# Linear attention on one core: a loop over groups becomes a loop over pairs, with work placed between the cells of an output

## The chip, the cores and the metric

The kernel runs on one core of a Trainium2 chip. The core has a matrix engine (TensorE, PE in the profile), a vector engine (VectorE, DVE), a scalar engine (ScalarE, ACT), a general engine (GpSimd, POOL) and a sync engine (SyncE, SP) that here only issues DMAs. Each engine works through its own list of instructions in order and waits on semaphores for the others. The metric is the device time of one execution in microseconds (us); the number quoted is a median of runs.

## The reference

```python
batch, heads, seq, dim = 8, 12, 512, 64      # Q, K, V: float32

Q_feat = np.maximum(0, Q) + 1
K_feat = np.maximum(0, K) + 1
KV = np.einsum('bhkd,bhkv->bhdv', K_feat, V)
K_sum = np.sum(K_feat, axis=2)
numerator = np.einsum('bhqd,bhdv->bhqv', Q_feat, KV)
denominator = np.einsum('bhqd,bhd->bhq', Q_feat, K_sum)
return (numerator / (denominator[:, :, :, None] + 1e-10)).astype(np.float32)
```

There are 96 heads. For each, a 64 x 64 matrix KV and a 64-vector K_sum are summed over 512 keys, and then every one of 512 queries is multiplied with both and divided.

## The kernel before

**Tiling.** The 49152 rows of Q, K and V are cut into 12 groups (`NG`), numbered 0 to 11; two neighbouring groups, an even one and the odd one behind it, form a pair, and there are six pairs. Loads convert from float32 to bf16 on the way in. From the second pair on, K, V and Q of a pair come as one DMA each, and each of the three has two buffers (`IN_BUFS`), so the load for pair s+2 waits until pair s has been read out of its buffer. All these loads and ten of the twelve stores are issued by GpSimd, in the order of the program; the stores of groups 10 and 11 are issued by SyncE, group 11's in five pieces (`store`, lines 133 to 150). The outputs of a pair share one of five buffers `o_sb`; the first load of Q also uses one.

**The steps for one group.** *k features* and *q features* (`feature`, line 153): max(x+1, 1) on VectorE, two instructions each. *V blocks* (`v_blocks`, lines 164 to 172): four copies of V, each multiplied with a 0/1 mask column, so that heads that share a tile stay apart; VectorE makes two and a half of the four (three instructions, line 170), ScalarE one and a half (two instructions, line 172). *Keys-values* (`keys_values`, line 194): 64 matmuls of k features with V blocks into psum tiles `kva_ps`. These sum over the pair, and behind the odd group four *kva copies* on ScalarE (line 207) bring them to bf16 in SBUF. *Transposes* (`transposes`, line 220): 16 on TensorE, eight to each of two psum tiles `qt_ps`, of which there are two in all; two *qt copies* (line 223) bring them to SBUF. The transposes of the even group fill columns 0 to 3 of the pair's `qt` tile, those of the odd group columns 4 to 7. *Output* (`out_matmuls`, line 233): per group two halves h, each with two output tiles `o_ps` of eight matmuls; the first tile of a half reads columns 0 to 3 of `qt`, the second 4 to 7, so both groups of a pair need the transposes of both. There are two `o_ps` tiles in all. *Norms* (`norms`, lines 250 and 251): VectorE takes the reciprocals of the denominators and multiplies, 48 times each in the whole kernel.

**What sets the order.** The order is written by hand: inside `tc.manual_schedule()` each engine executes what concerns it in the order of the program text, and the framework only adds the semaphore waits. The loop at line 290 runs over groups 0 to 9; groups 10 and 11 are written out at lines 310 to 327. In a round for an even group a stand k features and V blocks of a, the output of a-2, q features of a and of a+1, and keys-values of a. In the round for the odd group b = a+1 stand the transposes and qt copies of a, k features and V blocks of b, the output of a-1, the transposes and qt copies of b, keys-values of b and the kva copies. GpSimd's DMA issues for the next pair but one come behind the odd group; the stores begin with the round for group 7.

Of the kernel before, what the change touches and what calls it, by code (L numbers as in the profile page):

```python
# [19 lines left out]
def kernel(  # L20
# [27 lines left out]
    W = 2 * D1  # L48
# [31 lines left out]
    raw = {}  # L80
    bufs = {}
    kfs = {}
    qfs = {}
    qts = {}
    outs = {}
    cells_of = {}
    kva_ps = {}

    def load_first_q():
# [38 lines left out]
    def load_pair(s):  # L128
        load("k", (2 * s, 2 * s + 1))
        load("v", (2 * s, 2 * s + 1))  # L130
        load_q(s)
# [25 lines left out]
    def k_features(g):  # L157
        k_raw = raw.pop(("k", g))
        kf = kf_pool.tile([P, C2, 2, D], BF16, name="kf")
        for n in range(2):  # L160
            feature(kf[:, :, n], k_raw[:, n])
        kfs[g] = kf

    def v_blocks(g):
        v_raw = raw.pop(("v", g))
        for b in range(4):
            block = v_all[:, g % 2, :, :, b, 0:D]
            cut = 2 if b < 2 else 1 if b == 2 else 0
            if cut > 0:
                nc.vector.tensor_scalar_mul(block[:, 0:cut], v_raw[:, 0:cut], mask[:, b : b + 1])  # L170
            if cut < 2:
                nc.scalar.mul(out=block[:, cut:], in_=v_raw[:, cut:], mul=mask[:, b : b + 1])  # L172

    def q_features(g):
        q_raw = raw.pop(("q", g))
        qf = qf_pool.tile([P, R, C // 2, 2, D], BF16, name="qf")
        for n in range(2):
            feature(qf[:, :, :, n], q_raw[n])
        qfs[g] = qf

    def keys_values(g):
        kf = kfs.pop(g)
        if g % 2 == 0:
            kva_ps[g // 2] = [psum_kva.tile([P, BANK], FP32, name="kva_ps") for _ in range(2)]
        halves = kva_ps[g // 2]
        for c in range(C2):
            for n in range(2):
                if g < 2:
                    eight, first, last_c = g, (c, n) == (0, 0), (c, n) == (C2 - 1, 1)
                else:  # L190
                    eight, first, last_c = n, g % 2 == 0 and c == 0, g % 2 == 1 and c == C2 - 1
                for h in range(2):
                    ps = slice(64 * h, 64 * h + 64)
                    nc.tensor.matmul(  # L194
                        halves[h][64 * eight : 64 * eight + 64, 0 : 4 * DV],
                        lhsT=kf[ps, c, n, :],
                        rhs=v_all[ps, g % 2, n, c],
                        start=first,
                        stop=last_c,
                    )  # L200
        if g % 2 == 0:
            return
        for h in range(2):
            kva = kva_diag[(g - 1 + h) % NV]
            for n in range(2):
                ps = slice(64 * n, 64 * n + 64)
                nc.scalar.copy(  # L207
                    out=kva[ps, :, n, :],
                    in_=halves[h][ps, 0 : 4 * DV].rearrange("p (b x) -> p b x", b=4)[:, :, 0:D1],
                )  # L210

    def transposes(g):
        qf = qfs.pop(g)
        if g % 2 == 0:
            qts[g // 2] = mid_pool.tile([P, C, P, R], BF16, name="qt")
        for half in range(2):
            qt_ps = psum_qt.tile([P, 2, R, P], BF16, name="qt_ps")
            for c in range(2):
                for r in range(R):
                    nc.tensor.transpose(qt_ps[:, c, r], qf[:, r, 2 * half + c, :, :], identity)  # L220
            copy = nc.vector.tensor_copy if half and g == NG - 2 else nc.scalar.copy
            lo = g % 2 * 4 + 2 * half
            copy(out=qts[g // 2][:, lo : lo + 2], in_=qt_ps.rearrange("p c r q -> p c q r"))  # L223

    def out_matmuls(g, h):
        qt = qts[g // 2]
        kva = kva_diag[(g // 2 * 2 + h) % NV]
        ops = [psum.tile([P, 2, BANK], FP32, tag="ps", name="o_ps") for _ in range(2)]
        for c in range(C):
            for j in range(2):  # L230
                b = 2 * (g % 2) + j
                q = 16 * (4 * h + b)
                nc.tensor.matmul(  # L233
                    ops[c // 4][64 * j : 64 * j + 64, c // 2 % 2, (c % 2) * W : (c % 2) * W + W],
                    lhsT=qt[:, c, q : q + 16, :],
                    rhs=kva[:, b],
                    start=True,
                    stop=True,
                )
        cells_of[g, h] = ops  # L240

    def norms(g, h):
        ops = cells_of.pop((g, h))
        if (g % 2, h) == (0, 0):
            outs[g // 2] = out_pool.tile([P, 2 * NP, C, D], FP32, name="o_sb")
        o_sb = outs[g // 2]
        for i in range(2):
            cells = ops[i][:, :, 0 : 2 * W].rearrange("p b (c n x) -> p b c n x", n=2, x=D1)
            recip = recip_pool.tile([P, 2, 2, 2, 1], FP32, name="recip")
            nc.vector.reciprocal(out=recip, in_=cells[:, :, :, :, D:D1])  # L250
            nc.vector.tensor_tensor(  # L251
                out=o_sb[:, 2 * h + g % 2 : 2 * NP : NP, 4 * i : 4 * i + 4].rearrange(
                    "p n (b c) d -> p b c n d", b=2
                ),
                in0=cells[:, :, :, :, 0:D],
                in1=recip.to_broadcast([P, 2, 2, 2, D]),
                op=ALU.mult,
            )

    def output(g):  # L260
        for h in range(2):
            out_matmuls(g, h)
            norms(g, h)

    with tc.manual_schedule():
        q_first = load_first_q()
        load("k", (0,))
        load("v", (0,))
        load_rest_q(q_first)
        load("k", (1,))  # L270
        load("v", (1,))
        make_identity(nc, identity)
        nc.vector.tensor_reduce(  # L273
            out=mask,
            in_=identity.rearrange("p (h b x) -> p b h x", h=2, b=4),
            op=ALU.add,
            axis=mybir.AxisListType.XY,
        )
        for i in range(2):
            t = v_all[:, i].rearrange("p n c b x -> p (n c) b x")  # L280
            nc.vector.memset(t[:, :, :, D1:], 0.0)
            nc.vector.tensor_copy(  # L282
                out=t[:, :, :, D], in_=mask[:, None, :].to_broadcast([P, 2 * C2, 4])
            )
        for t in kva_diag:
            for b in range(4):
                nc.gpsimd.memset(t[:, b], 0.0)  # L287
        load_pair(1)
        last = NG - 1
        for g in range(last - 1):  # L290
            if g % 2:
                transposes(g - 1)
            k_features(g)
            v_blocks(g)
            if g >= 2:
                output(g - 2)
            if g % 2:
                transposes(g)
            else:
                q_features(g)  # L300
                q_features(g + 1)
            keys_values(g)
            if g % 2 and g // 2 + 2 < NG // 2:
                load_pair(g // 2 + 2)
            if g == NG - 5:
                for done in range(g - LAG):
                    store(done)
            if g >= NG - 5:
                store(g - LAG)
        k_features(last - 1)  # L310
        output(last - 3)
        out_matmuls(last - 2, 0)
        v_blocks(last - 1)
        k_features(last)
        v_blocks(last)
        keys_values(last - 1)
        store(last - 1 - LAG)
        q_features(last - 1)
        q_features(last)
        norms(last - 2, 0)  # L320
        transposes(last - 1)
        out_matmuls(last - 2, 1)
        norms(last - 2, 1)
        transposes(last)
        keys_values(last)
        output(last - 1)
        output(last)
        for g in range(last - LAG, NG):
            store(g)


# [28 lines left out]
```

## Time and profile before

| | |
|---|---|
| time, median of 3 runs | 126.53 us (126.38 to 130.75) |
| profiled execution | 126.8 us, span 125.0 us |
| TensorE, matmuls | 72.0 us busy, 58% of the span |
| VectorE | 82.4 us, 66% |
| ScalarE | 67.8 us, 54% |
| GpSimd | 24.6 us, 20% |
| HBM traffic | 37.75 MB read, 12.58 MB written: 403 GB/s over the span |
| keys-values matmuls (line 194) | 768, mean 340 ns |
| V blocks on ScalarE (line 172) | 24, mean 1572 ns |
| qt copies on ScalarE (line 223) | 23, mean 1016 ns |
| kva copies (line 207) | 24, mean 374 ns |
| norms on VectorE (lines 250, 251) | 48 of 199 ns and 48 of 692 ns |

The span is the time from the first to the last event of one profiled execution; the device time includes what lies around it, here 1.8 us. The page divides the span into 40 slices of 3.1 us and gives the busy share of each engine in each slice as a digit in tenths; for TensorE there is a second row with the clock that was granted, in tenths of full speed. The chain that ended last is followed back from the last instruction, at each step to what released it. The timeline lists merged instructions with start and length; in square brackets stands how long the engine had been idle before and what ended that.

### The profile page before, as it was taken

How to read it: one execution, taken by the hardware profiler on the slowest of the kernel's cores; microseconds unless marked ns; L12 is line 12 of the kernel's file. 1: busy time of each engine (PE TensorE's matmuls, PEld its weight loads, DVE VectorE, ACT ScalarE, POOL GpSimd, SP SyncE). 2: the span in 40 equal slices, each digit the busy share in tenths (PEclk: the TensorE clock that was granted, in tenths of full speed). 3: DMA queues.
4: the chain of work that ended last, by engine and by line, in shares of the span. 5: the costliest groups of instructions: out<-in, count | busy, mean ns of one | idle time of the engine just before them, and what ended most of it. 6: DMA issues, size and time to landing. Idle time of an engine off the chain costs nothing.

```text
span 125.0 us, 3095 instructions
## 1 busy us (share of the span) xinstructions
PE 72.0 (58%) x1344; PEld 60.9 (49%) x1344; DVE 82.4 (66%) x186; ACT 67.8 (54%) x72; POOL 24.6 (20%) x52
## 2 busy tenths in 40 slices
PE   0000297389549474696737967449767459974500
PEld 0000296289338463684626847348656337763300
DVE  0466642205299996969959769599290999939920
ACT  0006703970673989329994099870698990571000
POOL 6990020040002050020400203950201020020000
PEclk9999999855999999769995599965799955999655
DMA  3999999999999999999999999999999999999892
GB/s 86 339 214 210 219 211 216 214 211 219 211 215 215 216 212 215 215 218 214 211 218 214 211 221 208 215 215 215 216 372 414 413 418 418 409 415 413 337 372 101
DMA packets 8902, 32.18 MB, mean 257 GB/s; under 512 B 568, under 2 KB 824, under 8 KB 8760
## 3 DMA queue, kind: packets, MB, share of 16 engines
q0 software_dynamic: 7520, 28.84, 93.7%
q1 hardware_dynamic: 1368, 3.15, 7.0%
q8 instruction: 10, 0.16, 0.5%
q14 instruction: 4, 0.03, 0.1%
HBM read 37.75 MB, written 12.58 MB: 403 GB/s over the span
## 4 chain that ended last, share of the span: by engine, by line
ACT 37%; PE 33%; DVE 15%; DMA 7%; issue 3%; POOL 1%; ACTq 0%; POOLq 0%
PE kva_ps L194 28%; ACT v_all L172 24%; ACT qt L223 8%; DVE o_sb L251 7%; DMA v_raw<-in_V_dram 7%; ACT kva_all L207 4%; PE qt_ps L220 4%; DVE v_all L170 3%; DVE recip L250 2%; DVE qf L153 1%; ACT L172 1%; DVE qt L223 1%; PE o_ps L233 1%; DVE kf L153 1%; POOL k_raw L113 1%
## 5 line engine op out<-in xcount | busy, mean ns | idle before, releaser
L194 PE MATMUL kva_ps<-v_all,kf 64*64 64x272 bf16 x768 | 39.1, 340 | 25.4 <-ACT v_all L172 24.1
L194 PEld LDWEIGHTS <-kf 64*64 64x64 bf16 x768 | 35.2, 132 | 27.0 <-DVE v_all L170 13.9
L223 ACT COPY qt<-qt_ps 128x1024 bf16<-128x1024 bf16 x23 | 22.2, 1016 | 27.2 <-PE qt_ps L220 27.2
L172 ACT ACTIVATE v_all<-v_raw,mask 128x1024 bf16<-128x1024 bf16 (+1 forms) x24 | 36.4, 1572 | 0.1
L251 DVE TENSOR_TENSOR o_sb<-o_ps,recip 128x512 f32<-128x512 f32 x48 | 33.2, 692 | 1.6
L233 PE MATMUL o_ps<-kva_all,qt 128*64 128x130 bf16 x384 | 19.3, 233 | 20.1 <-DVE recip L250 7.6
L170 DVE TENSOR_SCALAR v_all<-v_raw,mask 128x2048 bf16<-128x2048 bf16 (+1 forms) x36 | 22.7, 688 | 8.5 <-DMA v_raw<-in_V_dram 8.5
L233 PEld LDWEIGHTS <-qt 128*64 128x64 bf16 x384 | 13.3, 114 | 26.3 <-DVE o_sb L251 10.6
L250 DVE RECIPROCAL recip<-o_ps 128x8 f32<-128x8 f32 x48 | 9.6, 199 | 17.3 <-PE o_ps L233 17.3
L220 PE MATMUL qt_ps<-identity,qf 128*128 128x128 bf16 x192 | 14.8, 235 | 1.1 <-ACT qt L223 1.0
L220 PEld LDWEIGHTS <-qf 128*128 128x128 bf16 x192 | 12.4, 106 | 4.0 <-issue 3.1
L207 ACT CAST kva_all<-kva_ps 64x260 bf16<-64x260 f32 x24 | 9.0, 374 | 7.4 <-PE kva_ps L194 7.1
L137 POOL DMA_DIRECT2D out_dram<-o_sb x10 | 7.5, 763 | 25.3 <-DVE o_sb L251 20.5
L153 DVE TENSOR_SCALAR kf<-k_raw 128x1024 bf16<-128x1024 bf16 x24 | 9.1, 422 | 4.7 <-DMA k_raw<-in_K_dram 4.7
L110 POOL DMA_DIRECT2D k_raw<-in_K_dram x5 | 3.6, 727 | 33.8 <-DVE kf L153 33.8
L110 POOL DMA_DIRECT2D v_raw<-in_V_dram x5 | 4.0, 793 | 26.6 <-ACT v_all L172 26.6
L153 DVE TENSOR_SCALAR qf<-q_raw 128x1024 bf16<-128x1024 bf16 x22 | 8.0, 419 | 0.1
L172 ACT ACT_TABLE_LOAD x1 | 1.3, 1283 | 10.5 <-DMA v_raw<-in_V_dram 10.5
L123 POOL DMA_DIRECT2D q_raw<-in_Q_dram x5 | 3.6, 720 | 0.0
L273 DVE TENSOR_REDUCE mask<-identity 128x4 f32<-128x128 bf16 x1 | 0.3, 286 | 4.7 <-POOL identity masks.py:199 4.7
L287 POOL MEMSET kva_all<- 128x130 bf16 x16 | 2.4, 196 | 0.0
L282 DVE CAST v_all<-mask 128x128 bf16<-128x128 f32 x2 | 2.2, 1637 | 0.0
(12 smaller groups left out, 7.2 us busy)
## 6 DMA issues: line engine op xcount, KB each, us to landing
out_dram<-o_sb POOLq DMA_DIRECT2D x10, 1024.0 KB, 20.2
k_raw<-in_K_dram POOLq DMA_DIRECT2D x5, 1024.0 KB, 14.2
v_raw<-in_V_dram POOLq DMA_DIRECT2D x5, 1024.0 KB, 13.5
q_raw<-in_Q_dram POOLq DMA_DIRECT2D x5, 1024.0 KB, 17.2
o_sb<-in_Q_dram SPq DMA_DIRECT2D x1, 1024.0 KB, 4.8
k_raw<-in_K_dram POOLq DMA_DIRECT2D x2, 512.0 KB, 9.5
v_raw<-in_V_dram POOLq DMA_DIRECT2D x2, 512.0 KB, 11.4
out_dram<-o_sb SPq DMA_DIRECT2D x1, 1024.0 KB, 5.3
```

The lines of the kernel that those rows point to most:

```text
L110: nc.gpsimd.dma_start(out=t, in_=drams[x][:, 2 * s : 2 * s + 2])
L137: nc.gpsimd.dma_start(out=o_to[:, g % 2 : 2 * NP : 2], in_=outs[s][:, g % 2 : 2 * NP : 2], single_packet=True)
L153: nc.vector.tensor_scalar(out=dst, in0=src, scalar1=1.0, scalar2=1.0, op0=ALU.add, op1=ALU.max)
L170: nc.vector.tensor_scalar_mul(block[:, 0:cut], v_raw[:, 0:cut], mask[:, b : b + 1])
L172: nc.scalar.mul(out=block[:, cut:], in_=v_raw[:, cut:], mul=mask[:, b : b + 1])
L194: nc.tensor.matmul(halves[h][64 * eight : 64 * eight + 64, 0 : 4 * DV], lhsT=kf[ps, c, n, :], rhs=v_all[ps, g % 2, n, c], start=first, sto ...
L207: nc.scalar.copy(out=kva[ps, :, n, :], in_=halves[h][ps, 0 : 4 * DV].rearrange("p (b x) -> p b x", b=4)[:, :, 0:D1],)
L220: nc.tensor.transpose(qt_ps[:, c, r], qf[:, r, 2 * half + c, :, :], identity)
L223: copy(out=qts[g // 2][:, lo : lo + 2], in_=qt_ps.rearrange("p c r q -> p c q r"))
L233: nc.tensor.matmul(ops[c // 4][64 * j : 64 * j + 64, c // 2 % 2, (c % 2) * W : (c % 2) * W + W], lhsT=qt[:, c, q : q + 16, :], rhs=kva[:, ...
L250: nc.vector.reciprocal(out=recip, in_=cells[:, :, :, :, D:D1])
L251: nc.vector.tensor_tensor(out=o_sb[:, 2 * h + g % 2 : 2 * NP : NP, 4 * i : 4 * i + 4].rearrange("p n (b c) d -> p b c n d", b=2), in0=cell ...
```

## The change

The loop over groups becomes a loop over pairs (`iteration`). The copies that followed a step inside its function (`kva copies`, `qt copies`) become functions of their own, `v_blocks` takes the engine as an argument, and `output` issues its four tiles one by one, with room for other work between them: behind the first two tiles of the output of the preceding odd group stand the transposes and qt copies of the even group, behind the third tile a quarter of the keys-values matmuls of the odd group. The q features of the odd group move behind that output and behind its own keys-values matmuls. The k features and V blocks of the next even group are issued at the end of a round; the qt copies of the preceding odd group are issued at the start of the next. In the last pair (`end`) the k features and V blocks of group 11 come first, and the qt copies of group 10 are issued behind the kva copies. The qt copy that VectorE made for group 10 is made by ScalarE. Stores 0 to 5 are issued behind the fourth pair's round, 6 and 7 behind the fifth's, 8 and 9 behind the sixth's.

```diff
-    def keys_values(g):
-        kf = kfs.pop(g)
-        if g % 2 == 0:
+    def keys_values(g, lo=0, hi=C2):
+        kf = kfs[g]
+        if g % 2 == 0 and lo == 0:
             kva_ps[g // 2] = [psum_kva.tile([P, BANK], FP32, name="kva_ps") for _ in range(2)]
         halves = kva_ps[g // 2]
-        for c in range(C2):
+        for c in range(lo, hi):
...
-        if g % 2 == 0:
-            return
+
+    def keys_values_copies(s):
+        halves = kva_ps[s]
         for h in range(2):
-            kva = kva_diag[(g - 1 + h) % NV]
+            kva = kva_diag[(2 * s + h) % NV]
...
+        qt_ps[g] = [psum_qt.tile([P, 2, R, P], BF16, name="qt_ps") for _ in range(2)]
         for half in range(2):
-            qt_ps = psum_qt.tile([P, 2, R, P], BF16, name="qt_ps")
             for c in range(2):
                 for r in range(R):
-                    nc.tensor.transpose(qt_ps[:, c, r], qf[:, r, 2 * half + c, :, :], identity)
-            copy = nc.vector.tensor_copy if half and g == NG - 2 else nc.scalar.copy
+                    nc.tensor.transpose(qt_ps[g][half][:, c, r], qf[:, r, 2 * half + c, :, :], identity)
+
+    def transpose_copies(g):
+        for half, t in enumerate(qt_ps.pop(g)):
             lo = g % 2 * 4 + 2 * half
-            copy(out=qts[g // 2][:, lo : lo + 2], in_=qt_ps.rearrange("p c r q -> p c q r"))
+            nc.scalar.copy(out=qts[g // 2][:, lo : lo + 2], in_=t.rearrange("p c r q -> p c q r"))
...
+    def output(g, between=()):
+
+        cells = [(g, h, i) for h in range(2) for i in range(2)]
+        for k in range(4):
+            if k >= 2:
+                norms(*cells[k - 2])
+                if k - 2 < len(between):
+                    between[k - 2]()
+            out_matmuls(*cells[k])
+        norms(*cells[2])
+        norms(*cells[3])
+
+    def iteration(s):
+
+
+        a, b = 2 * s, 2 * s + 1
+        end = b == NG - 1
+        quarter = C2 // 4
+        if end:
+            k_features(b)
+            v_blocks(b, "dve")
+            v_blocks(b, "act")
+        transpose_copies(a - 1)
+        output(a - 2)
+        q_features(a)
+        if end:
+            q_features(b)
+        else:
+            k_features(b)
+            v_blocks(b, "dve")
+            v_blocks(b, "act")
+        keys_values(a)
+
+        def first():
+            transposes(a)
+            if not end:
+                transpose_copies(a)
+
+        output(a - 1, (first, lambda: keys_values(b, 0, quarter)))
+        keys_values(b, quarter, C2)
+        if not end:
+            q_features(b)
+        keys_values_copies(s)
+        if end:
+            transpose_copies(a)
+        transposes(b)
+        if end:
+            transpose_copies(b)
...
+        blocks(0)
+        keys_values(0)
+        q_features(0)
+        q_features(1)
+        transposes(0)
+        blocks(1)
+        transpose_copies(0)
+        keys_values(1)
+        keys_values_copies(0)
+        transposes(1)
+        load_pair(2)
+        blocks(2)
+        for s in range(1, NG // 2):
+            iteration(s)
+            if s + 2 < NG // 2:
+                load_pair(s + 2)
+            if 2 * s + 2 < NG:
+                blocks(2 * s + 2)
+            for g in range(2 * s - 2, 2 * s) if s > 3 else range(2 * s) if s == 3 else ():
+                store(g)
+        output(NG - 2)
+        output(NG - 1)
+        for g in range(NG - 2, NG):
             store(g)
```

`blocks(g)` calls `k_features(g)`, `v_blocks(g, "dve")` and `v_blocks(g, "act")`.

More of the change, by code (lines that the diff above doesn't have):

```diff
@@ L86 @@
     cells_of = {}
+    qt_ps = {}
     kva_ps = {}
@@ L162, in k_features, with v_blocks @@
         kfs[g] = kf
-    def v_blocks(g):
-        v_raw = raw.pop(("v", g))
+    def v_blocks(g, engine):
+        v_raw = raw["v", g]
         for b in range(4):
@@ L168, in v_blocks @@
             cut = 2 if b < 2 else 1 if b == 2 else 0
-            if cut > 0:
+            if engine == "dve" and cut > 0:
                 nc.vector.tensor_scalar_mul(block[:, 0:cut], v_raw[:, 0:cut], mask[:, b : b + 1])
-            if cut < 2:
+            if engine == "act" and cut < 2:
                 nc.scalar.mul(out=block[:, cut:], in_=v_raw[:, cut:], mul=mask[:, b : b + 1])
@@ L215, in transposes, with out_matmuls @@
             qts[g // 2] = mid_pool.tile([P, C, P, R], BF16, name="qt")
+        qt_ps[g] = [psum_qt.tile([P, 2, R, P], BF16, name="qt_ps") for _ in range(2)]
         for half in range(2):
-            qt_ps = psum_qt.tile([P, 2, R, P], BF16, name="qt_ps")
             for c in range(2):
                 for r in range(R):
-                    nc.tensor.transpose(qt_ps[:, c, r], qf[:, r, 2 * half + c, :, :], identity)
-            copy = nc.vector.tensor_copy if half and g == NG - 2 else nc.scalar.copy
+                    nc.tensor.transpose(qt_ps[g][half][:, c, r], qf[:, r, 2 * half + c, :, :], identity)
+    def transpose_copies(g):
+        for half, t in enumerate(qt_ps.pop(g)):
             lo = g % 2 * 4 + 2 * half
-            copy(out=qts[g // 2][:, lo : lo + 2], in_=qt_ps.rearrange("p c r q -> p c q r"))
-    def out_matmuls(g, h):
+            nc.scalar.copy(out=qts[g // 2][:, lo : lo + 2], in_=t.rearrange("p c r q -> p c q r"))
+    def out_matmuls(g, h, i):
         qt = qts[g // 2]
         kva = kva_diag[(g // 2 * 2 + h) % NV]
-        ops = [psum.tile([P, 2, BANK], FP32, tag="ps", name="o_ps") for _ in range(2)]
-        for c in range(C):
+        o_ps = psum.tile([P, 2, BANK], FP32, tag="ps", name="o_ps")
+        for c in range(4 * i, 4 * i + 4):
             for j in range(2):
@@ L233, in out_matmuls @@
                 nc.tensor.matmul(
-                    ops[c // 4][64 * j : 64 * j + 64, c // 2 % 2, (c % 2) * W : (c % 2) * W + W],
+                    o_ps[64 * j : 64 * j + 64, c // 2 % 2, (c % 2) * W : (c % 2) * W + W],
                     lhsT=qt[:, c, q : q + 16, :],
@@ L239, in out_matmuls @@
                 )
[L240 to L244, printed above, removed]
-            outs[g // 2] = out_pool.tile([P, 2 * NP, C, D], FP32, name="o_sb")
[L246 to L263, printed above, removed]
+        cells_of[g, h, i] = o_ps
+    def norms(g, h, i):
+        cells = cells_of.pop((g, h, i))[:, :, 0 : 2 * W].rearrange(
+            "p b (c n x) -> p b c n x", n=2, x=D1
+        )
+        if (g % 2, h, i) == (0, 0, 0):
+            outs[g // 2] = out_pool.tile([P, 2 * NP, C, D], FP32, name="o_sb")
+        recip = recip_pool.tile([P, 2, 2, 2, 1], FP32, name="recip")
+        nc.vector.reciprocal(out=recip, in_=cells[:, :, :, :, D:D1])
+        nc.vector.tensor_tensor(
+            out=outs[g // 2][:, 2 * h + g % 2 : 2 * NP : NP, 4 * i : 4 * i + 4].rearrange(
+                "p n (b c) d -> p b c n d", b=2
+            ),
+            in0=cells[:, :, :, :, 0:D],
+            in1=recip.to_broadcast([P, 2, 2, 2, D]),
+            op=ALU.mult,
+        )
@@ L265, with blocks @@
+    def blocks(g):
+        k_features(g)
+        v_blocks(g, "dve")
+        v_blocks(g, "act")
     with tc.manual_schedule():
@@ L288 @@
         load_pair(1)
[L289 to L328, printed above, removed]
+        blocks(0)
[21 more added lines that the diff above has]
+        for g in range(NG - 2, NG):
             store(g)
```

## The prediction

> **What bounds the kernel now.** First the page's part 2, to see whether the transfers or the engines set the pace.
>
> ```profile
> PEclk9999999855999999769995599965799955999655
> DMA  3999999999999999999999999999999999999892
> GB/s 86 339 214 210 219 211 216 214 211 219 211 215 215 216 212 215 215 218 214 211 218 214 211 221 208 215 215 215 216 372 414 413 418 418 409 415 413 337 372 101
> ```
>
> The sixteen DMA engines are busy in every slice from the second to the thirty-seventh. Loads write 215 GB/s of bf16, that is 430 GB/s read, until about 91.3 us; then stores run at about 414 GB/s. Twelve stores of 1024 KB (1.049 MB) cost 2.53 us each, 30.4 us together, so transfers alone would end at 91.3 + 30.4 = 121.7 us. The span is 125.0. So there is a floor close beneath this kernel, and a second bound, the engines, that ends at nearly the same time. Next the chain that ended last, over one regular pair:
>
> ```profile
> 64.10 3.05 ACT v_all L172 x2
> 67.14 0.04 issue
> 67.19 3.84 PE kva_ps L194 x64
> 71.03 0.98 PE qt_ps L220 x8
> 72.01 0.02 issue
> 72.03 1.93 ACT qt L223 x2
> 73.96 2.95 ACT v_all L172 x2
> 76.91 0.04 issue
> 76.95 2.10 PE kva_ps L194 x64
> ...
> 80.21 0.38 ACT kva_all L207
> ```
>
> Columns: start, length, what. This is a loop between ScalarE and TensorE: V blocks of the even group, its 64 keys-values matmuls, the transposes, their two copies, V blocks of the odd group, its 64 matmuls, the four kva copies. It returns at 48.2, 64.1, 80.6 and 97.1 us, so a pair takes 16.5 us, against 3 x 4.88 = 14.6 us for its three loads (2.10 MB read each at 430 GB/s). Compute falls behind the loads and is the bound by the end. The timeline shows what lies beside the chain: the odd group's two qt copies run during its matmuls and cost nothing.
>
> ```profile
> 76.79 1.92 ACT L223 COPY qt<-qt_ps 128x1024 bf16<-128x1024 bf16 x2
> 76.95 2.05 PE L194 MATMUL kva_ps<-v_all,kf 64*64 64x272 bf16 x64 [0.73 <-ACT v_all L172]
> ...
> 118.80 0.69 DVE L251 TENSOR_TENSOR o_sb<-o_ps,recip 128x512 f32<-128x512 f32 x1
> 119.52 0.34 SPq L146 DMA_DIRECT2D out_dram<-o_sb  x1
> ```
>
> The last product ends at 119.5, and the pieces of the last store take 5.5 us from there to the end of the span.
>
> **The change, part by part.** No arithmetic goes or comes, except that one qt copy moves from VectorE (1.21 us) to ScalarE (1.01). What changes is the order on each in-order engine. ScalarE per pair now has: V blocks of the even group a (issued at the end of the round before), qt copies of the preceding odd group, V blocks of the odd group b, qt copies of a, kva copies. I call T the moment when the four kva copies of a pair end and follow one round from there; "cell" is an output tile of 8 matmuls (0.42), followed by a norm on VectorE of 0.84 (97.05 to 97.89).
>
> Round at the clock 1.00. ScalarE: V blocks of a to T+3.05, qt copies of a-1 to T+5.0 (0.96 each once both are pipelined). TensorE: cell 0 of group a-2 is early, since it needs only the kva copies and the even qt; cell 1 reads qt columns 4 to 7, the odd group's, so it waits until T+5.05. Norm 1 ends at T+6.2, cell 3 needs that psum tile and ends at T+6.65, and only behind it in TensorE's queue stand the matmuls of a. Before, they began at T+3.1. That is the added wait: 3.5 us, and the V blocks, done at T+3.05, wait for TensorE instead of the other way. Matmuls of a: 2.05, to T+8.7. Two cells of a-1: 0.65, T+9.35. Sixteen transposes: 1.07, T+10.4. VectorE meanwhile has norms 2 and 3 to T+7.85, q features 0.71, k features 0.67, V blocks 1.8: T+11.05; then norm 0 to T+11.9, which releases cell 2, T+12.4; a quarter of b's matmuls 0.51, T+12.9; cell 3, T+13.3 (norm 1 done at T+12.75); the other three quarters 1.54, T+14.85; kva copies 1.55 and 0.05 to start: T+16.45. Removed from the chain, in exchange: V blocks of b (2.95) now end at T+8.0, and qt copies of a run beside cells and matmuls. So the round is 16.45 at full clock, no gain on 16.5, though before's round had its first 64 matmuls at 3.84.
>
> The clock decides what is added to that. In the trace TensorE fell to 0.50 at about 24.4 after an idle stretch from 23.3, and near 65.5, 82.6 and 99.5 after the sparse output cells; it came back 3.3 to 5.5 us after dense matmuls began. In the new round TensorE does nothing from about T+0.2 to T+4.05. I take the half clock for a's matmuls alone: 3.84 brings them to T+10.5, cells T+11.15, transposes T+12.2, cell 2 T+12.65, and the round 16.7; with half of the transposes slowed too, 16.9, which I use. Bounds: 16.45, nothing slow; 19.1, everything slow (1.62 for transposes, 3.84 for both groups).
>
> The Trainium skill ("TensorE: Matmul & The Clock Gate", section "What's actually happening") says that the array's clock is halved after an idle window of about 3.4 us and released after as long a busy one. The new round's 3.85 us of idleness per pair would by that rule make a's matmuls slow in every round, where the chain of before had one round of 14.35 without it; the rule speaks against this change, and the stretches named above partly bear it out, since the clock there fell after less idleness. By it the sum is the forecast's; without it, the full-clock rival's.
>
> Start. The V blocks of group 1 no longer wait behind the qt copies of group 0: ScalarE runs them when their load is in, 17.9 to 20.9, not 22.5 to 25.5. The 64 matmuls follow at 21.1 (6.63, as slow as before) to 27.7, kva copies to 29.3. The next V blocks need the load that before had at 28.79, so T of pair 0 is 29.0, where it was 33.8: 4.8 us earned. Four rounds of 16.9 give T of pair 4 = 96.6; before had 97.1. The head start is spent.
>
> End. Before, this T to the last norm took 22.4 us (97.1 to 119.5). Now: V blocks of 10 and of 11 stand on ScalarE ahead of the qt copies of 9: 5.97 + 1.93, T+7.9. Cell 1, norm 1 and cell 3 of group 8 then end at T+9.55 (before, its matmuls of 10 began at T+5.15). Matmuls 3.84: T+13.4. Two cells T+14.05, transposes 1.07 T+15.1, cell 2 T+15.5, quarter T+16.0, cell 3 T+16.45, rest T+18.0, kva copies T+19.6. The qt copies of 10 stand behind these: 1.93, T+21.55; only they free the psum tiles for the transposes of 11, T+22.1, whose copies end at T+23.5. Before, both pairs of copies lay ahead of the kva copies. Cell 1 of group 10 needs the last copy: its norm ends T+24.7, two more norms T+26.4, four of group 11 T+29.75. Bounds: 28.0 at full clock, 31.6 at half.
>
> Sum: 96.6 + 29.75 = 126.35 for the last product, +5.5 for the store pieces = 131.85 span. The profiled execution took 126.8 around a span of 125.0, 1.8 outside: 133.65. It stands 0.27 above the median of the runs, 126.53, so **133.4** on the median's scale.
>
> Moved DMAs. GpSimd's order of loads stays. K of pair 5 is issued after k features of 7, at T(2)+9.2 = 72.0 (before 69.6); the engines need it at 91.3 - 14.6 = 76.7, so it is covered. Q of pair 5 now waits for q features that come after a whole output: T(2)+15.2 = 78.0, before 77.9; queued behind it are stores 0 to 5, needed at 91.3. Were that cover gone, each us late would be a us of idle transfers, but the end would not see it while compute ends at 126. Store 8 is issued near T+10.8 = 107.4, store 9 near 114.5, stores 10 and 11 on SP after their norms. The output buffer of group 10 needs stores 0 and 1 landed, near 98; its norms come at 119.
>
> **The rivals.** Full clock: with 16.45 and 28.0 the last product comes at 29.0 + 65.8 + 28.0 = 122.8, time 129.8. For it: matmuls spread over the round; against: the idle 3.85 us. Colder: rounds of 17.5 and an end of 31 give 130.0, time 137. For it: the clock needed up to 5.5 us of dense work to return, and cells break the dense run.
>
> The other side, **the transfer floor**: the 4.8 us earned at the start are kept because a round is no longer than its loads. Then compute follows the loads, the stores never lack data, and the end is 121.7 plus about 1.8 of landing and closing: span 123.5, time 125.0, not slower. It decides if the last product comes by 118, so T(4) by 88.3, rounds of 14.8. For it: before's first round took 14.35 at full clock, and VectorE's work per pair is only 13.1 us. Against: the wait for the odd qt copies and norm 1 ahead of the matmuls. That the order isn't as written is excluded, since the instruction lists of both kernels show it.
>
> The Trainium skill ("DMA: Bandwidth & Descriptors", section "Where 436 GB/s comes from") puts the ports' ceiling at about 435 GB/s and HBM's share per core at about 358; the loads here read 430, so the first agrees and the second doesn't. By 435 the 50.3 MB take 115.7 us, an estimate, and the floor rival would fall by some 2.8 us (88.1 of loads and 30.4 of stores in the rows).
>
> **How the numbers follow.** Forecast (131 to 136) 0.56; full clock (129 to 131) 0.14; colder (over 136) 0.12; the head start and the tail nearly cancel (124.5 to 128.5, the floor rival and part way to it) 0.14; below that 0.04. About 2% is what a measurement of this kernel can tell from no change: 124.0 to 129.1. Faster 0.04, within 0.13, slower 0.83. The range reaches from 128.5, under the full-clock end, to 137.5, past colder.
>
> **What would show it.** Right: kva copies end near 29 and then every 16.5 to 17.5 us; before the matmuls of even groups TensorE waits for ScalarE's qt copies and VectorE's norms, not V blocks; the four last qt copies end some 4 us behind the last kva copies; transfers idle after about 114; the last product near 126. Wrong: rounds of 15 or less, or cell 1 not waiting for the odd copies; then the stores end last.

## The result and the profile after

The changed kernel takes 135.1 us (median of four executions, 134.07 to 136.45). The ratio to the kernel before is 1.066, 95% interval 1.054 to 1.077: slower. The profiled execution took 134.07 us around a span of 132.3, where before it was 126.8 around 125.0. Some executions run 2 to 3.5% longer than the others of the same kernel (before up to 130.75 us, against 126.38); ratios here compare executions without that, while the times are medians of all.

Part 2 of the page of the changed kernel, as shown of before:

```profile
PEclk9999999985569995599955999558996557977755
DMA  3999999999999999999999999999999999570492
GB/s 111 316 208 217 216 212 212 214 217 216 214 217 207 219 214 214 216 211 214 216 214 216 212 217 213 214 218 284 419 417 417 417 416 410 223 307 0 165 381 91
```

The loads run as before. The stores begin as before too, but now the transfers run dry: half a slice of work at 112 to 116 us, and nothing at all in the slice around 120. The engines, which had ended level with the transfers, end behind them. The windows of this profile between the ends of the kva copies of one pair and the next, and then to the last product (columns: stretch, its length, TensorE busy, its weight loads, VectorE, ScalarE, GpSimd, granted clock, DMA share, GB/s):

```profile
26.98:45.63 18.65, 11.19 (x224) 8.55 (x224) 13.73 (x32) 11.33 (x12) 2.15 (x3) 0.73 1.06 215
45.63:62.46 16.83, 11.23 (x224) 8.60 (x224) 12.94 (x31) 11.33 (x12) 2.15 (x3) 0.80 1.06 214
62.46:79.18 16.72, 11.21 (x226) 8.66 (x224) 12.89 (x31) 11.32 (x12) 2.45 (x4) 0.80 1.06 215
79.18:96.08 16.90, 11.61 (x230) 8.66 (x224) 13.43 (x31) 11.33 (x13) 6.12 (x8) 0.80 1.05 271
96.08:116.17 20.09, 10.36 (x202) 7.86 (x201) 11.85 (x28) 9.40 (x11) 1.51 (x2) 0.75 0.94 383
116.17:126.71 10.54, 6.10 (x80) 4.20 (x79) 6.62 (x16) 3.87 (x4) 0.00 (x0) 0.72 0.43 173
```

Where the 7.3 us of span come from can be read off these six rows and the profile of before. The first kva copies end at 27.0 instead of 33.8. Four rounds later the lead is down to 1.0 us (96.1 against 97.1). The last pair takes 20.1 us where before it took 15.9 (97.1 to 113.0): 4.2 lost. From the last kva copies to the last product it is 10.5 where it was 6.5 (113.0 to 119.5): 4.0 lost. The store pieces take 5.6 us behind the last product, before 5.5. Together -1.0 + 4.2 + 4.0 + 0.1 = 7.3. The last kva copies of before, in its timeline:

```profile
111.41 1.54 ACT L207 CAST kva_all<-kva_ps 64x260 bf16<-64x260 f32 x4 [0.82 <-PE kva_ps L194]
```

What fills a round shows in the chain that ended last, here the round that began at 62.46 (start, length, what; the rows "issue" between them, 0.02 to 0.04 us each, are left out):

```profile
62.48 3.04 ACT v_all L173 x2
65.54 1.94 ACT qt L227 x2
67.52 0.45 PE o_ps L237 x4
67.99 0.22 DVE recip L253
68.24 0.70 DVE o_sb L254
68.98 0.65 PE o_ps L237 x8
69.63 3.60 PE kva_ps L195 x59
```

V blocks of the even group, then the qt copies of the odd group before, then the second half of the second output cell, its norm, the fourth cell, and only then the matmuls of the even group: they begin 7.1 us after the kva copies, although their V blocks were ready 4.0 us earlier. Before, matmuls came directly behind the V blocks. In the other three of the four rounds the chain takes another way from the same late cell: behind its norm on VectorE stand two more norms, the q and k features and VectorE's V blocks, and only then the norm that frees the tile for the next cell. From the round that began at 45.63:

```profile
53.77 0.67 DVE qf L154 x2
54.44 0.67 DVE kf L154 x2
55.11 1.90 DVE v_all L171 x3
...
57.99 0.42 PE o_ps L237 x8
```

Both ways start at the qt copies. The list of waits of the changed kernel says the same (who waited for whom: total us, times, longest):

```profile
PE o_ps L237 <- ACT qt L227: 28.3, 11, 7.1
...
PE kva_ps L195 <- ACT v_all L173: 15.1, 1, 15.1
```

The second line is the wait at the very start alone; before, there were ten of that kind, the one at the start among them:

```profile
PE kva_ps L194 <- ACT v_all L172: 24.1, 10, 14.9
```

The last pair of the changed kernel, in the timeline:

```profile
96.11 5.97 ACT L173 ACTIVATE v_all<-v_raw,mask 128x1024 bf16<-128x1024 bf16 x4
...
103.17 0.43 PE L237 MATMUL o_ps<-kva_all,qt 128*64 128x130 bf16 x4 [7.07 <-ACT qt L227]
...
116.18 1.93 ACT L227 COPY qt<-qt_ps 128x1024 bf16<-128x1024 bf16 x2
117.24 1.93 PE L222 MATMUL qt_ps<-identity,qf 128*128 128x128 bf16 x16 [2.65 <-ACT qt L227]
118.27 1.95 ACT L227 COPY qt<-qt_ps 128x1024 bf16<-128x1024 bf16 x2 [0.17 <-PE qt_ps L222]
```

With four V block instructions instead of two ahead of the qt copies, TensorE stands for 7.1 us. Behind the last kva copies (to 116.17) come four qt copies with the transposes of group 11 between them, and only at 120.2 is the tile complete that the last outputs read.

### The profile page after: what moved, and what is told of

Read it like the earlier page. It is cut to its first block, busy times and chain, and to the rows that moved or that the text cites. A ratio compares the mean times of both kernels' runs of the same rounds, so it can differ in the third digit from the quotient of the medians.

```text
span 132.3 us, 3089 instructions
## 1 busy us (share of the span) xinstructions
PE 73.3 (55%) x1344; PEld 57.3 (43%) x1344; DVE 82.3 (62%) x185; ACT 69.4 (52%) x73; POOL 24.6 (19%) x52
## 4 chain that ended last, share of the span: by engine, by line
ACT 26%; DVE 24%; PE 22%; DMA 16%; POOL 5%; issue 3%; ACTq 0%; POOLq 0%
DMA v_raw<-in_V_dram 16%; ACT v_all L173 14%; DVE o_sb L254 13%; PE kva_ps L195 12%; ACT qt L227 8%; PE o_ps L237 6%; ACT kva_all L209 4%; DVE v_all L171 4%; PE qt_ps L222 3%; DVE recip L253 3%; DVE qf L154 2%; POOL kva_all L339 2%; DVE kf L154 2%; POOL k_raw L114 1%; POOL v_raw L114 1%
## 5 line engine op out<-in xcount | busy, mean ns | idle before, releaser
L237 PE MATMUL o_ps<-kva_all,qt 128*64 128x130 bf16 x384 | 23.7, 263 | 33.7 <-ACT qt L227 28.3
L195 PEld LDWEIGHTS <-kf 64*64 64x64 bf16 x768 | 30.6, 134 | 20.1 <-DVE v_all L171 12.5
L237 PEld LDWEIGHTS <-qt 128*64 128x64 bf16 x384 | 15.2, 130 | 42.2 <-ACT qt L227 30.6
L227 ACT COPY qt<-qt_ps 128x1024 bf16<-128x1024 bf16 x24 | 23.1, 1015 | 16.2 <-PE qt_ps L222 15.9
L222 PE MATMUL qt_ps<-identity,qf 128*128 128x128 bf16 x192 | 13.7, 227 | 3.6 <-ACT qt L227 2.6
L222 PEld LDWEIGHTS <-qf 128*128 128x128 bf16 x192 | 11.5, 101 | 5.9 <-issue 3.3
L154 DVE TENSOR_SCALAR qf<-q_raw 128x1024 bf16<-128x1024 bf16 x22 | 8.5, 430 | 0.1
L173 ACT ACT_TABLE_LOAD x1 | 1.3, 1283 | 10.7 <-DMA v_raw<-in_V_dram 10.7
```

The costliest lines, as they stand in the source:

```text
L154: nc.vector.tensor_scalar(out=dst, in0=src, scalar1=1.0, scalar2=1.0, op0=ALU.add, op1=ALU.max)
L195: nc.tensor.matmul(halves[h][64 * eight : 64 * eight + 64, 0 : 4 * DV], lhsT=kf[ps, c, n, :], rhs=v_all[ps, g % 2, n, c], start=first, sto ...
L222: nc.tensor.transpose(qt_ps[g][half][:, c, r], qf[:, r, 2 * half + c, :, :], identity)
L227: nc.scalar.copy(out=qts[g // 2][:, lo : lo + 2], in_=t.rearrange("p c r q -> p c q r"))
L237: nc.tensor.matmul(o_ps[64 * j : 64 * j + 64, c // 2 % 2, (c % 2) * W : (c % 2) * W + W], lhsT=qt[:, c, q : q + 16, :], rhs=kva[:, b], sta ...
```

## The experiments

Two theories were set against each other. *The queue*: the loss is the qt copies' place on ScalarE, and TensorE's order, which puts cells that wait for those copies ahead of matmuls that could run. No run changes TensorE's order by itself; that part is argued from the waits. *The clock*: the loss is TensorE's fall to half clock behind the idle stretches that the new order opens. In the table, the last three columns are of the profiled execution.

| run | time, us | ratio to before (95%) | clock | last product | span |
|---|---|---|---|---|---|
| before, page shown above | 126.53 | 1 | 0.843 | 119.5 | 125.0 |
| changed | 135.1 | 1.066 (1.054 to 1.077) | 0.801 | 126.7 | 132.3 |
| qt copies first in each round | 126.29 | 1.000 (0.999 to 1.001) | 0.821 | 113.7 | 124.5 |
| qt copies of group 10 first | 131.77 | 1.044 (1.037 to 1.050) | 0.808 | 125.3 | 130.9 |
| both moves | 126.30 | 1.000 (0.999 to 1.001) | 0.828 | 112.6 | 124.5 |
| unread matmuls, 7 times | 135.24 | 1.072 (1.064 to 1.079) | 0.816 | 127.3 | 132.9 |
| unread matmuls, 16 times | 133.50 | 1.059 (1.051 to 1.067) | 0.890 | 126.6 | 132.1 |
| last pair mended | 130.34 | 1.033 (1.030 to 1.036) | 0.814 | 121.3 | 126.9 |
| before with the new start | 126.43 | 0.999 (0.998 to 1.000) | 0.885 | 113.3 | 124.7 |
| changed with the old start | 139.90 | 1.109 (1.102 to 1.115) | 0.808 | 131.4 | 137.0 |
| both moves, stores from GpSimd | 127.59 | 1.011 (1.009 to 1.013) | 0.826 | 112.8 | 126.0 |
| changed, once more | 134.53 | 1.063 (1.052 to 1.074) | | | |

**The qt copies of the odd group ahead of the next V blocks.** On ScalarE alone, the order of two steps is exchanged:

```diff
-        transpose_copies(a - 1)
         output(a - 2)
...
         transposes(b)
-        if end:
-            transpose_copies(b)
+        transpose_copies(b)
...
         transposes(1)
+        transpose_copies(1)
         load_pair(2)
```

> The changed kernel with one thing moved: the two qt copies of an odd group are issued right behind its transposes, so on ScalarE they stand ahead of the V blocks of the next even group instead of behind them. Theory of the queue: the second output cell of a round can run at T+2.0 instead of T+4.1 to T+5.0, the matmuls of the even group wait for nothing but their V blocks, which now end at T+5.0, and begin there instead of at T+7.1. From there 9.7 us to the end of the round as measured: rounds of 14.7, or what the loads allow (14.6); the last pair can begin when its V is in, about 88, and the last product comes at 112 to 116. The end is then the transfer floor, span about 123.5, time about 125, ratio to before 0.98 to 1.0. Theory of the clock: the output cells remain sparse, TensorE still falls to 0.50, and the rounds stay above 16; time 131 to 134, ratio 1.03 to 1.05.

Measured: 126.29 us, the loss gone, the last product at 113.7. The rounds, in the windows of this run:

```profile
42.58:57.87 15.29, 12.06 (x224) 9.78 (x224) 13.20 (x30) 11.21 (x13) 2.15 (x3) 0.78 1.06 214
57.87:72.47 14.60, 10.93 (x226) 8.96 (x224) 12.92 (x30) 11.21 (x13) 2.58 (x4) 0.88 1.06 214
```

The first of them ran at a granted clock of 0.78, lower than the 0.80 of the changed kernel's rounds, and was still 1.5 us shorter than those. So it is the queue. Rounds of 14.3 (72.47 to 86.74) and 14.6 are what the loads allow: VectorE's V blocks then wait seven times for their data (13.1 us), where they waited three times in the changed kernel (8.2 us). In the last pair this move also puts the qt copies of group 9 ahead of the V blocks of group 11, so it mends one of the two places that are tested apart below. The time, though, isn't the 125 that was expected but 126.3, and the ratio is 1: products end 13 us earlier than in the changed kernel, 5.8 earlier than before, and the end comes 0.5 us before that of the kernel before (124.5 against 125.0 in the profiles). The tail is taken up below.

**The last pair's qt copies ahead of the last kva copies.**

```diff
         def first():
             transposes(a)
-            if not end:
-                transpose_copies(a)
+            transpose_copies(a)
...
-        if end:
-            transpose_copies(a)
         transposes(b)
```

> The changed kernel with one thing moved in the last pair alone: the qt copies of group 10 are issued behind its transposes, as in all other pairs, and so stand ahead of the last kva copies on ScalarE. Theory of the queue: the transposes of group 11 find free psum tiles and run beside the last kva copies, their qt copies follow these directly, and the last cells come 1.9 us earlier: last product near 124.8, time 1.9 us below the changed kernel's, ratio to before about 1.05. Rival: VectorE's eight norms set the end anyway, and it gains under 0.5 us.

Measured: 131.77 us. From the end of the last kva copies to the last product 8.3 us (117.0 to 125.3) instead of 10.5, so 2.2 us are regained, a little over the 1.9. The changed kernel's ratio of 1.063 to 1.066 falls to 1.044. Its timeline shows the transposes of group 11 beside the kva copies, as expected:

```profile
115.35 1.07 PE L222 MATMUL qt_ps<-identity,qf 128*128 128x128 bf16 x16
115.46 1.55 ACT L209 CAST kva_all<-kva_ps 64x260 bf16<-64x260 f32 x4 [1.32 <-PE kva_ps L195]
...
117.03 1.93 ACT L227 COPY qt<-qt_ps 128x1024 bf16<-128x1024 bf16 x2
```

The transposes also took 1.07 us instead of 1.93: TensorE had not stood idle for 2.65 us before them. In the changed kernel the last copies waited 0.17 us for the slow ones, which is part of the difference to the 1.9.

**The last pair mended in both places.** The second move, with the one above; rounds and start stay as changed:

```diff
         if end:
             k_features(b)
             v_blocks(b, "dve")
-            v_blocks(b, "act")
         transpose_copies(a - 1)
+        if end:
+            v_blocks(b, "act")
         output(a - 2)
```

> The changed kernel with the last pair alone mended: the qt copies of group 10 ahead of the last kva copies (as in the run with that alone), and the V blocks of group 11 behind the qt copies of group 9 on ScalarE instead of ahead of them. Rounds and beginning as changed. Theory of the queue: the second output cell of group 8 comes 2.95 us earlier, and everything behind it; from the kva copies of the fifth pair to the last product 30.6 less 2.2 less 2.95 = 25.5 us, time 5 us below the changed kernel's, ratio 1.02 to 1.03. Theory of the clock: the idle stretch of the last pair falls from 7.1 to 4.1 us but the matmuls behind it stay at 0.50, and only the 2.2 us are gained.

Measured: from the fifth pair's kva copies to the last product 25.2 us (96.13 to 121.33), expected 25.5, against 30.6 in the changed kernel. The matmuls of group 10 ran at half clock here as there (3.82 and 3.84 us for the 64), so the 5 us are the two places in ScalarE's queue. Of the 8.2 us that the last pair lost against before, 5.4 are regained; the other 2.8 (25.2 against 22.4) were not taken apart. The time is 130.34 and the ratio 1.033, where the changed kernel has 1.063 on the same chip: 3.9 us less, short of the 5 expected, though the profiled spans differ by 5.4 (126.9 against 132.3; this profile is of the run's quickest execution).

**Both moves, in every round and in the last pair** (the first two diffs together).

> Both moves together, of the odd group's qt copies in every round and of group 10's in the last pair. Theory of the queue: the last product comes at 110 to 114, but the stores can't end sooner than about 121.7, so the time is that of the first move alone, about 125, within 0.5 us. Theory of the clock: rounds above 16, and 1.9 us less than with the first move alone, 129 to 132.

Measured: 126.30 us, the same as with the first move alone, although the last product comes 1.1 us earlier. The engines no longer set the end.

**Filling the idle stretch, first attempt.** Ahead of the second cell of an even group the same eight cells are computed from columns that are ready:

```diff
         o_ps = psum.tile([P, 2, BANK], FP32, tag="ps", name="o_ps")
+        if g % 2 == 0 and (h, i) == (0, 1) and g < NG - 2:
+            for _ in range(15 if g == NG - 4 else 7):
+                for c in range(4, 8):
+                    for j in range(2):
...
+                        nc.tensor.matmul(o_ps[...], lhsT=qt[:, c - 4, q : q + 16, :], rhs=kva[:, b], start=True, stop=True)
```

> The changed kernel with added matmuls that nobody reads: ahead of the second output cell of groups 0, 2, 4, 6 and 8, TensorE computes the same eight cells from columns 0 to 3 of qt, 7 times (15 times for group 8), into the tile that the real matmuls then overwrite; results are unchanged. They fill the idle 3.9 us (7.1 in the last pair), and the clock should stay at 1.00 for the matmuls of the even group (2.05 us instead of 3.7 to 3.84). Theory of the queue: these still begin at T+6.65, and behind them VectorE's features and norms take over the chain, so a round falls from 16.8 to 16.4 only and the end by 1.7 to 2.4; together 2 to 4 us, time about 132, ratio 1.03 to 1.05. Theory of the clock: every round gets the 2.3 us back that its matmuls and cells lose at half clock, and the end as much and more; together 9 to 12 us, time 123 to 126, ratio below 1.0.

Measured: 135.24 us, no gain, and it doesn't decide between the theories. The 56 unread matmuls took 1.75 us instead of the 3.9 they were to fill, 2.5 us of idleness were left, and the clock fell as before (the matmuls of group 6 took 3.84 us).

**Filling it whole.** The same with 16 and 28 instead of 7 and 15.

> The changed kernel with the unread matmuls ahead of the second output cell of the even groups again, now 16 times eight (28 times for group 8): each takes 31 ns at full clock as measured, so they fill the whole idle stretch, 4.0 and 7.0 us, where 7 and 15 times eight had left 2.5 us idle and the clock had fallen all the same. If the clock now stays at 1.00 for the matmuls of the even group: theory of the queue: VectorE takes the chain over, since its features follow the third and fourth norm and end 0.1 us sooner than before, so the rounds stay within 0.4 of 16.8, and only the last pair gains, 2 to 3 us: time 132 to 133, ratio 1.04 to 1.05. Theory of the clock: 2 us a round and more at the end, 9 us together: time 125 to 127, ratio near 1.0.

Measured: 133.50 us, where 132 to 133 were expected by the queue and 125 to 127 by the clock. The ratio is 1.059 against 1.063 of the changed kernel on the same chip; the intervals overlap, so no gain is shown. The clock was held throughout in one round only; the rounds around it had 0.90 and 0.91. That one is the test that was wanted; its window in this run:

```profile
45.55:62.27 16.72, 12.96 (x359) 10.95 (x354) 12.96 (x31) 11.33 (x13) 2.15 (x3) 1.00 1.06 215
```

The clock is 1.00 throughout, where the changed kernel's same round had 0.80 and took 16.83. A tenth of a microsecond is what the clock cost there. The two rounds behind it took 16.61 and 16.45 at 0.90, and with the qt copies of group 10 moved alone, where the rounds are as changed, they took 17.0 at 0.80. So the clock is worth a few tenths of a microsecond a round, not the 2 that its theory expects. The timeline of the run shows why:

```profile
52.31 2.04 PE L195 MATMUL kva_ps<-v_all,kf 64*64 64x272 bf16 x61
...
54.84 1.98 DVE L171 TENSOR_SCALAR v_all<-v_raw,mask 128x2048 bf16<-128x2048 bf16 x3
...
56.74 0.19 DVE L266 RECIPROCAL recip<-o_ps 128x8 f32<-128x8 f32 x1
...
57.81 0.42 PE L250 MATMUL o_ps<-kva_all,qt 128*64 128x130 bf16 x8 [1.05 <-DVE recip L266]
```

The 64 matmuls end at 55.2 (the last three behind a gap of 0.5 us), 9.6 us after the kva copies instead of 10.7, and then TensorE waits 1.05 us for a norm that stands on VectorE behind features and V blocks. In the changed kernel these same steps carried the chain of this round already. The gain of 2 to 3 us expected in the last pair did not come: there the unread matmuls themselves ran on to 105.7, past the moment when the qt copies were done (103.3), so the 64 matmuls of group 10, at full clock (2.11 us), ended when they had at half clock. For the last pair this run therefore decides nothing.

**The start alone, in the kernel before.**

```diff
+            if g == 1:
+                k_features(g)
+                v_blocks(g)
             if g % 2:
                 transposes(g - 1)
-            k_features(g)
-            v_blocks(g)
+            if g != 1:
+                k_features(g)
+                v_blocks(g)
```

> The kernel before with the beginning of the change alone: k features and V blocks of group 1 are issued ahead of the transposes and qt copies of group 0, so ScalarE doesn't hold the V blocks of group 1 back; all else as before. Theory of the queue: the kva copies of the first pair end at 30 to 32 instead of 33.8, the rounds keep their 16.5 and carry the head start to the end: last product at 116 to 117.5 instead of 119.5, time set by the transfers, 1 to 1.5 us below the kernel before, ratio 0.985 to 0.995. Rival: the loads set the pace of the middle, the rounds lengthen, and the head start is gone by the last pair: ratio 1.00.

Measured: the first kva copies end at 30.35, as expected, and the last product comes at 113.3, 2.7 us ahead of the range expected, since two of the old order's rounds kept the full clock and took 14.3 and 14.5 us (the two at 0.89 took 15.9). The time is 126.43, ratio 0.999, interval 0.998 to 1.000. Six us on the engines are worth a tenth of a per cent, which the interval does not tell from nothing: the rival, though not for its reason. The head start was not lost on the way, it met the transfers.

**The old start in the changed kernel.**

```diff
         transposes(0)
+        transpose_copies(0)
         blocks(1)
-        transpose_copies(0)
+        transposes(1)
         keys_values(1)
         keys_values_copies(0)
-        transposes(1)
```

> The changed kernel with its beginning undone: V blocks of group 1 behind the qt copies of group 0, and the transposes of group 1 ahead of its keys-values matmuls, as before; the rounds and the end as changed. Theory of the queue: the first kva copies end near 33.8, the next V blocks start there instead of at 28.8, and everything after comes 4 to 5 us later: last product at 131, time about 139.5, ratio 1.09 to 1.11. Rival: the loads set the pace of the rounds, and the time stays within 1 us of the changed kernel's.

Measured: 139.90 us, ratio 1.109; the first kva copies end at 33.6, the last product comes at 131.4. Where the engines set the end, the start's 4.7 us count whole. Loads were late too (139 to 169 GB/s in three slices between 61 and 82 us), and the end did not see it.

**Simpler last stores.** Both moves, and groups 10 and 11 stored like the others:

```diff
     def store(g):
...
-        if g < NG - 2:
-            nc.gpsimd.dma_start(...)
-            return
...
-        nc.sync.dma_start(out=o_to[:, 7, 0:cut], in_=o_sb[:, 7, 0:cut])
+        nc.gpsimd.dma_start(
+            out=o_to[:, g % 2 : 2 * NP : 2], in_=outs[s][:, g % 2 : 2 * NP : 2], single_packet=True
+        )
```

> Both moves (qt copies of the odd group ahead of the next V blocks in every round, and of group 10 ahead of the last kva copies), and the stores of groups 10 and 11 as one transfer each from GpSimd like the other ten, where SyncE had issued them in one and five pieces. With the moves alone, products end 11 us before the span, transfers run at full rate to 121 and then trickle for 2.5 us. Theory of the transfer floor: if the small pieces make the trickle, the span falls from 124.5 to about 123.5, ratio to before 0.99; if the sixteen engines just finish unevenly, it stays within 0.3 us and the ratio at 1.00.

Measured: 127.59 us, 1.1% longer, which neither theory had. The windows of this run at the end:

```profile
121.00:122.00 1.00, 0.00 (x0) 0.00 (x0) 0.00 (x0) 0.00 (x0) 0.00 (x0) 0.50 0.58 234
122.00:123.00 1.00, 0.00 (x0) 0.00 (x0) 0.00 (x0) 0.00 (x0) 0.00 (x0) 0.50 0.13 53
123.00:124.00 1.00, 0.00 (x0) 0.00 (x0) 0.00 (x0) 0.00 (x0) 0.00 (x0) 0.50 0.02 8
```

The bytes end no later than with SyncE's pieces (272, 59 and 6 GB/s in these three stretches with the first move alone), so the small pieces don't make the trickle. But the span lasts to 126.0 and not to 124.5: 2 us pass after the last byte, where it was about 1. The run changes the issuing engine and the number of pieces together, so which of the two costs this is open.

**The changed kernel once more**, beside the last three on the same chip.

> The changed kernel itself, unaltered, as the measure for the three beside it on the same chip: 134 to 135.5 us, ratio 1.06 to 1.07.

Measured: 134.53 us, ratio 1.063 (1.052 to 1.074).

No version was found that beats the kernel before. Those whose engines end early and whose stores are as before meet the same end of the transfers at a span of 124.5 to 124.7.

## Why the prediction was right

It forecast 133.4 us, 5.4% above the 126.53 from which it reckoned; measured were 135.1, and a ratio of 1.066. By its own execution it said a span of 131.85, and the profile has 132.3. The profiled execution was the quickest of the four; two of the others, undisturbed as well, have spans of 133.2 and 133.4, and where their further microsecond lies was not looked for.

- *The added wait ahead of the matmuls of the even group.* Right, and shown: with the copies moved, rounds shrank to what the loads allow, at the same clock. Forecast T+6.65 for the start, measured T+7.1 (69.56 for T = 62.46), since the cells themselves ran at half clock (0.65 instead of 0.42), which the sum left out.
- *The round.* 16.9 taken, 16.7 to 16.9 measured for the three behind the first. The way through it was as forecast at half clock in one of them; in the others VectorE's norms, features and V blocks carried the chain, as in the working at full clock. The first counts 18.65 from its kva copies, but 16.9 from the V load that it had to wait for, as the forecast had it.
- *The start.* It was said that the V load at 28.8 would hold the second pair, and so it was. The term for the 64 matmuls of group 1 was mis-sized: 6.63 at half clock taken, 3.9 at full clock measured (21.45 to 25.34), which the load hid.
- *The head start is spent.* Pair 4 at 96.6 forecast, 96.1 measured. With the old start the end came 4.7 us later, so it had been worth that much.
- *The end.* T+29.75 forecast for the last product, T+30.6 measured. The two places named, the V blocks of 11 and the qt copies of 10, were worth 3.2 and 2.2 us of it (25.2 us remain when both are mended). Short by 0.9: 0.5 of it lies ahead of the last kva copies (T+20.1, 19.6 forecast), with the cells of group 8 at half clock (0.65 instead of 0.42); 0.2 in the transposes of group 11, taken at full clock, which took 1.93 us; 0.2 in the last cells and norms.
- *Moved DMAs.* K of pair 5 at 72.2 (72.0), Q at 78.2 (78.0), store 8 at 107.5 (107.4), store 9 at 114.4 (near 114.5).
- *The clock.* That a's matmuls run at half clock was right: 3.5 to 3.8 us for the 64, 3.84 taken. The forecast put 0.45 us into the round for it, 0.2 of this for slow transposes; the transposes of the rounds took 1.07, so they were not slow. The round that held 1.00 took 16.72 with VectorE on the chain, so the full-clock working, 16.45, was too low by 0.27, in part because VectorE's V blocks took 1.9 to 2.0 us and not 1.8. Two errors cancel in the sum of 16.9, and that is in part luck. The rule of the Trainium skill ("TensorE: Matmul & The Clock Gate", section "What's actually happening") that an idle window of some 3.4 us halves the clock agrees with the changed kernel, 4.1 us idle (62.5 to 66.6) and 0.50 from there on. It isn't the whole: with the stretch filled, the run with 16 repetitions fell to 0.50 at 69 after 1.1 us of idleness and a few cells.
- *The transfer floor.* As a rival it was rightly given little, but its price was 1.0 us too low: span 123.5 said, 124.5 to 124.7 measured in three runs whose products end at 112.6 to 113.7. The term is the landing and closing behind 121.7, taken as 1.8 without a row for it; in those runs bytes trickle from 121 to 123.5 or so, and about another us follows. The profiled execution of before (125.0) stood 0.3 to 0.5 us above this floor; in the comparisons its undisturbed executions span 124.4 to 124.8 but for one of 125.2, so it stood at the floor, and a better order of its engines had nothing left to gain.

## What to carry to other kernels

When copies move out of a function, look where they land in the queue of the engine that makes them, and what the reader's own queue holds behind the reader: here a 1.9 us copy behind a 3.0 us step let 64 matmuls start only 4.0 us after their data was there. Compute the floor of the transfers with its tail from a run that has one, before hoping for gains from order; near the floor only losses can be measured. And a last round written out by hand wants its own walk through every queue: here the last pair lost 8.2 us by itself, and two moves in one queue regained 5.4.

## What the runs showed that had not been expected

A slower clock costs little where another engine has the chain: in the changed order a round took 16.72 at 1.00 and 16.83 at 0.80, both with VectorE on the chain. In the old order, where the chain goes to and fro between ScalarE and TensorE, a round takes 14.3 to 14.5 us at 1.00 and 15.9 at 0.89. Long runs of unread matmuls had gaps of 0.7 to 2.65 us for which the profile names no wait; their cause was not looked for. And last stores issued whole by GpSimd closed the program 1.5 us later than SyncE's pieces (span 126.0 against 124.5) with the bytes ended at the same time, 1.1% of this kernel's time.
